# The per-row numbers of two softmaxes combined through scalar operands instead of tensor operands, in a two-layer hybrid encoder

## The chip, the cores and the metric

The kernel runs on one core of a Trainium2 chip, as one program. The metric is the device time of one execution in microseconds; several executions are timed and the median is quoted. The profile is of one further execution. Its span runs from the first to the last instruction that the profiler saw, and its own time is a little longer than its span.

## The reference

A sequence of 1024 tokens of width 1024, with 16 meta tokens put in front (1040 rows, T in the kernel), goes through two layers. The first layer holds two attentions side by side, and the change touches the softmax of both.

```python
# attention A ("MLA", 8 heads): dense, every row sees all 1040 keys
s = einsum('bhqd,bhkd->bhqk', qb, k) * scale
p = softmax(s, axis=-1)
o = einsum('bhqk,bhkd->bhqd', p, v)

# attention B ("SWA", 8 heads, 2 of keys): 16 meta keys and a band of +-128 keys,
# and one learned logit per head, the sink, which takes part in the sum only
p = softmax(concatenate([s_sink, s_meta, s_band], axis=-1), axis=-1)
o_real = p[..., 1:1+N_META] @ v_m + p[..., 1+N_META:] @ v_b
```

The rest of the first layer is an input projection, low-rank projections for attention A, a gate, and an output projection. The second layer is an input projection, a convolution, two recurrent scans and an output projection.

## The kernel before

Everything is float32. A product is made on TensorE (PE) from split operands: each operand is rounded to a shorter type ("hi") and the remainder is kept ("lo"), and three matmuls (lo x hi, hi x lo, hi x hi) go into one sum. So most tensors exist as a pair, and the remainder is always a subtraction on VectorE (DVE), or on GpSimd (POOL) for weights.

The program is written as one sequence, and a scheduler places the instructions on each engine's queue by its own estimate of durations; each queue then runs strictly in the order that was fixed. The stages, by the profile's time: first projections to about 290 us; attention B from 290 to 590 us, with projections of later tiles filling PE in between; gates to 700 us; one half of the output projection, with the first scores of attention A, to 775 us; attention A from 775 to 1140 us; the other half of the output projection; then the second layer from about 1200 us.

**Attention B** (`Unit`, lines 650 to 751) works in 36 units: four pairs of heads by nine blocks of query rows, where the ninth block is the 16 meta rows of both heads in one tile. For each of the two heads of a unit, three matmuls put the scores into PSUM (`sps`), and a custom DVE instruction (L685) scales them, adds the mask, writes `sp` (in the code `pt`) and returns the row maximum in `smx`. `snm` is the negated maximum (L688). Then the exponential of sink minus maximum, `ses`, is made in two steps: a DVE subtraction (L690) and a ScalarE (ACT) exponential (L691). ACT takes the exponential of each head's scores (L694) and sums it into `ssm`. DVE adds `ses` to the sum (L696) and takes the reciprocal (L697). POOL normalises the 16 meta columns into `spm` (L700), DVE the others (L703). PE transposes the result (L718, L721), and then come the products with the values.

**Attention A** (`m_scores`, from line 908; `m_values`, from line 960) works on 8 heads by 9 blocks of rows, in four groups of blocks per head. The scores of one block fill three stretches of PSUM (`px` two, `py` one, L918). DVE takes the maximum of 784 columns and of 256 columns (L924, L925) into two columns of the small tile `mmx`. L926 takes the larger of these two columns and multiplies it by the negated scale of the row, `nsc`. ACT takes the exponential of both parts (L928), each with its sum in a column of `mmx`. L930 adds the two sums, L931 takes the reciprocal, and POOL normalises: L936 the meta columns (`mpm`), L939 the other 1024 (`p`). Then PE transposes `p` (L982), ACT and DVE split the transpose into `pth` (L988) and `ptl` (L989), and PE multiplies them with the values (`av`, L998). For the meta columns the same is `mpr` (L976, L977, L993). The next head is prepared meanwhile (`head_prep`, from line 834): POOL makes `kn` and `rkb` (L844, L845), DVE the remainders `qnl`, `qrl`, `knl`, `kr`, `vl`, `mvmr` (L848, L759, L855, L868), and `yal` when a head's output is split.

Of the kernel before, what the change touches and what calls it, by code (L numbers as in the profile page):

```python
# [10 lines left out]
AF = mybir.ActivationFunctionType  # L11
ALU = mybir.AluOpType
# [29 lines left out]
def trunk_kernel(ctx: ExitStack, tc: tile.TileContext, a: dict, out: bass.AP):  # L42
    nc = tc.nc
# [28 lines left out]
    def row(nm, tag, dt=F32, w=T):  # L72
        if tag == "X":
            return xapool.tile([P, T], dt, tag="X", name=nm)
        return sb["P"].tile([P, w], dt, tag=tag, name=nm, bufs=sb["cnt"][tag])
# [90 lines left out]
    def bank(nm, tag):  # L166
        return sb["ps"].tile([P, 512], F32, tag=tag, name=nm, bufs=sb["pcnt"][tag])
# [88 lines left out]
    for k in range(8):  # L256
        h = row("xh", "X", F32R)
# [68 lines left out]
    for e in range(2):  # L326
        ps = first[3 + e]
        r = row("ckr", "T")
# [48 lines left out]
    for e in range(3):  # L377
        ps = run(proj1(e))
        h = row("cqh", "c", F32R)
        lo = row("cql", "c", F32R)  # L380
        r = row("cqr", "T")
# [84 lines left out]
    for hf in range(2):  # L466
        wu = [split_w(a["uv"][hf, k], (512,), "wv") for k in range(2)]
        for i in range(9):
            c0, m = (0, NM) if i == 8 else (NM + P * i, P)
# [41 lines left out]
    nsc = const.tile([P, 8, 9], F32, name="nsc")  # L511
# [138 lines left out]
    class Unit:  # L650
# [5 lines left out]
        def scores(self):  # L656
            u, i = self.u, self.i
            kh, kl = KV[u // 2, "k"]
            qs, qmeta, sc = QQ[u]
            if i == 8:  # L660
                m, w, nh = 32, 144, 1
                k0, mask, self.blocks = 0, m_meta, [0]
                lhs = [(qmeta[:, 0], qmeta[:, 1])]
                scs = [sc[:32, 16:17]]
                sinks = vec[:32, V_SINKM + u:V_SINKM + u + 1]
            else:
                m, nh = P, 2
                qsl = slice(NM + P * i, NM + P * i + P)
                lhs = [(qs[r][0][:, qsl], qs[r][1][:, qsl]) for r in range(2)]
                scs = [sc[:, 8 * r + i:8 * r + i + 1] for r in range(2)]  # L670
                sinks = vec[:, V_SINK + 2 * u:V_SINK + 2 * u + 2]
                if i == 0:
                    k0, w, mask, self.blocks = 0, 288, m_first, [0, 1]
                elif i == 7:
                    k0, w, mask, self.blocks = 144 * 6, 288, m_mid[:, :288], [6, 7]
                else:
                    k0, w, mask, self.blocks = 144 * (i - 1), 432, m_mid, [i - 1, i, i + 1]
            self.m, self.nh = m, nh
            pt = self.pt = row("sp", "sp", w=864)
            mx = small.tile([P, 2], F32, tag="smx", name="smx")  # L680
            for r in range(nh):
                ps = bank("sps", "s")
                for pi, (q, k) in enumerate(((lhs[r][1], kh), (lhs[r][0], kl), (lhs[r][0], kh))):
                    nc.tensor.matmul(ps[:m, :w], q, k[:, k0:k0 + w], start=pi == 0, stop=pi == 2)
                nc.vector.tensor_tensor_reduce(pt[:m, 432 * r:432 * r + w], ps[:m, :w], mask, scs[r], sinks[:, r:r + 1],  # L685
                                               ALU.add, ALU.max, mx[:m, r:r + 1])
            nm = small.tile([P, 2], F32, tag="snm", name="snm")
            nc.vector.tensor_scalar(nm[:m, :nh], mx[:m, :nh], -1.0, None, ALU.mult)  # L688
            es = small.tile([P, 2], F32, tag="ses", name="ses")
            nc.vector.tensor_sub(es[:m, :nh], sinks, mx[:m, :nh])  # L690
            nc.scalar.activation(es[:m, :nh], es[:m, :nh], AF.Exp)  # L691
            sm = small.tile([P, 2], F32, tag="ssm", name="ssm")
            for r in range(nh):
                nc.scalar.activation(pt[:m, 432 * r:432 * r + w], pt[:m, 432 * r:432 * r + w], AF.Exp,  # L694
                                     bias=nm[:m, r:r + 1], accum_out=sm[:m, r:r + 1])
            nc.vector.tensor_add(sm[:m, :nh], sm[:m, :nh], es[:m, :nh])  # L696
            nc.vector.reciprocal(sm[:m, :nh], sm[:m, :nh])  # L697
            pm = self.pm = swa.tile([P, 2, 96], F32, tag="spm", name="spm", bufs=2)
            for r in range(nh):
                nc.gpsimd.tensor_scalar(pm[:m, r].rearrange("p (a b) -> p a b", a=3),  # L700
                                        pt[:m, 432 * r:432 * r + 32].unsqueeze(1).to_broadcast([m, 3, 32]),
                                        sm[:m, r:r + 1], 1.0, ALU.mult, ALU.mult)
                nc.vector.tensor_scalar(pt[:m, 432 * r + NM:432 * r + w], pt[:m, 432 * r + NM:432 * r + w],  # L703
                                        sm[:m, r:r + 1], None, ALU.mult)
# [203 lines left out]
    def m_scores(h, tiles, res, tag="p", pms=None):  # L908
        q, qq, k, kr = HD[h][:4]
        for i in tiles:  # L910
            c0, m = (0, NM) if i == 8 else (NM + P * i, P)
            s = slice(c0, c0 + m)
            seq = ((q[1], k[0]), (q[0], k[1]), (qq[1], kr), (qq[0], kr), (q[0], k[0]))
            px = psC.tile([P, 1024], F32, tag="px", name="px", bufs=2)
            py = bank("py", "py")
            for dst, d0, a0, a1 in ((px, 240, 0, 272), (px, 512, 272, 784), (py, 0, 784, 1040)):
                for pi, (l, r) in enumerate(seq):
                    nc.tensor.matmul(dst[:m, d0:d0 + a1 - a0], l[:, s], r[:, a0:a1], start=pi == 0, stop=pi == 4)  # L918
                yield 1.0 / (3 * len(tiles))
            mx = small.tile([P, 6], F32, tag="mmx", name="mmx")  # L920
            sc = msc[:m, h, i:i + 1]
            p_ = row("p", tag)
            parts = ((py[:m, 0:256], 784, 1040), (px[:m, 240:1024], 0, 784))
            nc.vector.reduce_max(mx[:m, 0:1], parts[1][0], axis=AX.X)  # L924
            nc.vector.reduce_max(mx[:m, 1:2], parts[0][0], axis=AX.X)  # L925
            nc.vector.scalar_tensor_tensor(mx[:m, 2:3], mx[:m, 0:1], mx[:m, 1:2], nsc[:m, h, i:i + 1], ALU.max, ALU.mult)  # L926
            for z, (ps, b0, b1) in enumerate(parts):
                nc.scalar.activation(p_[:m, b0:b1], ps, AF.Exp, bias=mx[:m, 2:3], scale=sc,  # L928
                                     accum_out=mx[:m, 3 + z:4 + z])
            nc.vector.tensor_add(mx[:m, 5:6], mx[:m, 3:4], mx[:m, 4:5])  # L930
            nc.vector.reciprocal(mx[:m, 5:6], mx[:m, 5:6])  # L931
            if pms is None:
                pm = mla.tile([P, 96], F32, tag="mpm", name="mpm", bufs=6)
            else:
                pm = pms[:, 96 * len(res):96 * len(res) + 96]
            nc.gpsimd.tensor_scalar(pm[:m].rearrange("p (a b) -> p a b", a=3),  # L936
                                    p_[:m, 0:32].unsqueeze(1).to_broadcast([m, 3, 32]),
                                    mx[:m, 5:6], 1.0, ALU.mult, ALU.mult)
            nc.gpsimd.tensor_scalar(p_[:m, NM:T], p_[:m, NM:T], mx[:m, 5:6], 1.0, ALU.mult, ALU.mult)  # L939
            res.append((m, p_, pm))  # L940

    RES = {(0, 0): []}
    early = m_scores(0, GR[0], RES[0, 0], "X", row("pms", "X"))
    for d in range(8):
        ps = parts_c("op")
# [74 lines left out]
    def score_stream():  # L1020
        for h in range(8):
            prep = head_prep(h + 1, kpe, mla) if h < 7 else iter(())
            for gi in range(4):
                if h + gi:
                    res = RES[h, gi] = []
                    yield from m_scores(h, GR[gi], res)
                else:
                    yield from early
                if h + gi:
                    next(prep, None)  # L1030
            for _ in prep:
                pass
# [472 lines left out]
```

## Time and profile before

| | |
|---|---|
| time, median of 3 runs | 1940.13 us (1939.22 to 1945.82) |
| profiled execution, own time | 1936.07 us |
| its span | 1934.3 us |
| PE busy | 1828.5 us, 95% |
| DVE busy | 1278.4 us, 66% |
| ACT busy | 827.9 us, 43% |
| POOL busy | 943.9 us, 49% |
| granted TensorE clock, mean | 0.986 |

In a row of instructions, `x72: 202/220/2376` means 72 instructions with a shortest, a median and a longest duration in ns. In a row of groups, `| 35.8, 534 | 0.7` means 35.8 us busy in all, 534 ns for one on average, and 0.7 us in which the engine sat idle just before them. In a row of the timeline the first two numbers are start and duration in us, and square brackets give the idle time before the instruction and what ended it.

### The profile page before, as it was taken

Reading aid. Unit: us, or ns where it says so; the run is one execution under the profiler, and the core shown is the slowest. Engines: PE = TensorE matmul, PEld = TensorE weight load, DVE = VectorE, ACT = ScalarE, POOL = GpSimd, SP = SyncE. Lnnn points to the kernel's source line nnn. Section 1 sums busy time; section 2 is a strip of 40 time slices with the busy share of each in tenths; the row PEclk is TensorE's granted clock in tenths of the full one; section 3 lists DMA queues with packets and bytes.
Section 4 is the critical chain, followed back from the end, with each engine's and each line's share of the span. In section 5 each row is a group of like instructions: output and inputs, shape, how many; then the busy total and the mean of one; then the engine's idle time right before and its main releaser. Section 6 shows DMA issues by size and latency. Waiting matters only on the chain.

```text
span 1934.3 us, 28455 instructions
## 1 busy us (share of the span) xinstructions
PE 1828.5 (95%) x10822; PEld 1659.4 (86%) x10822; DVE 1278.4 (66%) x1953; ACT 827.9 (43%) x1366; POOL 943.9 (49%) x780
## 2 busy tenths in 40 slices
PE   8999989998999999999999999999999899988999
PEld 7988988888999999788878999988888788876887
DVE  7686358787663432889888753368898989893000
ACT  5455224444342201666666642155656464652000
POOL 5455355535224652544433333358676777655331
PEclk9999999999999999999999999999999999998999
DMA  5256532222223451323221014312222222246521
GB/s 180 73 184 232 132 84 65 64 75 72 78 75 122 143 194 57 113 73 92 69 70 55 18 47 160 106 50 71 82 67 81 84 69 88 66 157 232 183 82 44
DMA packets 111062, 192.77 MB, mean 100 GB/s; under 512 B 32143, under 2 KB 51727, under 8 KB 110926
## 3 DMA queue, kind: packets, MB, share of 16 engines
q1 hardware_dynamic: 110926, 190.96, 31.4%
q8 instruction: 85, 1.39, 0.3%
q14 instruction: 51, 0.42, 0.1%
HBM read 129.86 MB, written 53.06 MB: 95 GB/s over the span
## 4 chain that ended last, share of the span: by engine, by line
PE 53%; DVE 20%; POOL 9%; issue 9%; DMA 5%; ACT 4%; SPq 1%; DVEq 0%; ACTq 0%; POOLq 0%
PE pj L159 10%; PE oo L159 8%; PE pxop L159 6%; PE px L918 4%; PE av L998 4%; PE op L159 3%; PE up L159 3%; PE tp L982 3%; PE vps L426 2%; DVE tz L1243 2%; DMA wr<-in_wg 2%; POOL oz L1253 2%; POOL wl L107 2%; DVE oxc L1167 2%; PE pg L1143 2%
## 5 line engine op out<-in xcount | busy, mean ns | idle before, releaser
L106 POOL TENSOR_SCALAR wh<-wr 128x512 fp32r<-128x512 f32 (+2 forms) x219 | 196.3, 897 | 396.4 <-PE pj L159 99.0
L107 POOL TENSOR_TENSOR wl<-wr,wh 128x512 fp32r<-128x512 f32 (+2 forms) x219 | 352.6, 1610 | 17.5
L159 PE MATMUL pj<-xh,wl 128*128 128x346 f32 (+1 forms) x768 | 251.8, 328 | 12.3 <-DVE wl L107 7.2
L159 PE MATMUL pj<-xl,wh 128*128 128x346 f32 (+1 forms) x768 | 249.3, 325 | 0.7 <-DVE xl L260 0.6
L159 PE MATMUL pj<-xh,wh 128*128 128x346 f32 (+1 forms) x768 | 248.9, 324 | 0.0
L159 PEld LDWEIGHTS pj<-xh,wl 128*128 128x128 f32 x768 | 146.6, 191 | 14.2 <-ACT xh L259 7.1
L159 PEld LDWEIGHTS pj<-xl,wh 128*128 128x128 f32 x768 | 146.7, 191 | 2.2 <-DVE xl L260 2.1
L159 PEld LDWEIGHTS pj<-xh,wh 128*128 128x128 f32 x768 | 146.6, 191 | 0.1
L936 POOL TENSOR_SCALAR mpm<-p,mmx 128x96 f32<-128x96 f32 (+1 forms) x69 | 25.7, 372 | 209.2 <-DVE mmx L931 119.9
L1143 PE MATMUL pu<-h1h,wl 128*128 128x346 f32 (+1 forms) x384 | 125.5, 327 | 0.8 <-POOL wh L106 0.8
L1143 PE MATMUL pu<-h1l,wh 128*128 128x346 f32 (+1 forms) x384 | 124.9, 325 | 0.0
L1143 PE MATMUL pu<-h1h,wh 128*128 128x346 f32 (+1 forms) x384 | 124.8, 325 | 0.0
L988 ACT CAST pth<-tp 128x512 fp32r<-128x512 f32 (+1 forms) x160 | 78.9, 506 | 83.4 <-PE tp L982 82.0
L1294 DVE TENSOR_TENSOR hres<-oo,hres 128x512 f32<-128x512 f32 x16 | 10.6, 687 | 151.6 <-PE oo L159 151.6
L989 DVE TENSOR_TENSOR ptl<-tp,pth 128x512 fp32r<-128x512 f32 (+1 forms) x160 | 91.9, 583 | 23.3 <-ACT pth L988 21.7
L159 PE MATMUL oo<-oyl,wh 128*128 128x512 f32 x256 | 102.3, 400 | 4.4 <-DMA oyl<-s_yl 4.4
L159 PE MATMUL oo<-oyh,wl 128*128 128x512 f32 x256 | 100.3, 401 | 3.3 <-DMA oyh<-s_y 3.3
L159 PE MATMUL oo<-oyh,wh 128*128 128x512 f32 x256 | 102.7, 402 | 0.0
L1143 PE MATMUL pg<-h1h,wl 128*128 128x512 f32 x256 | 101.4, 396 | 0.0
L1143 PE MATMUL pg<-h1h,wh 128*128 128x512 f32 x256 | 101.1, 395 | 0.0
L1143 PE MATMUL pg<-h1l,wh 128*128 128x512 f32 x256 | 100.8, 394 | 0.0
L982 PE MATMUL tp<-ident,p 128*128 128x128 f32 (+1 forms) x576 | 96.2, 274 | 0.0
(446 smaller groups left out, 5564.5 us busy)
## 6 DMA issues: line engine op xcount, KB each, us to landing
wr<-in_w SPq DMA_DIRECT2D x128, 256.0 KB
wr<-in_wo SPq DMA_DIRECT2D x64, 256.0 KB
s_y<-oyh SPq DMA_DIRECT2D x14, 512.0 KB
s_yl<-oyl SPq DMA_DIRECT2D x14, 512.0 KB
oyh<-s_y SPq DMA_DIRECT2D x14, 512.0 KB
oyl<-s_yl SPq DMA_DIRECT2D x14, 512.0 KB
s_g<-gth SPq DMA_DIRECT2D x10, 520.0 KB
xr<-in_x SPq DMA_DIRECT2D x8, 520.0 KB
```

The costliest lines, as they stand in the source:

```text
L106: eng.tensor_scalar(hi[:, :n], raw[:, :n], 1.0, 1.0, ALU.mult, ALU.mult)
L107: eng.tensor_sub(lo[:, :n], raw[:, :n], hi[:, :n].bitcast(F32))
L159: nc.tensor.matmul(t[:, :c1 - c0], w, x[:, c0:c1], start=first and j == 0 and pi == 0, stop=last and j == nt - 1 and pi == 2)
L426: nc.tensor.matmul(ps[:m, :n], s, w, start=j == 0 and pi == 0, stop=j == nt - 1 and pi == 2)
L918: nc.tensor.matmul(dst[:m, d0:d0 + a1 - a0], l[:, s], r[:, a0:a1], start=pi == 0, stop=pi == 4)
L982: nc.tensor.transpose(tp[:, o:o + m], p_[:m, NM + P * (kt + j):NM + P * (kt + j) + P], ident[:m, :m])
L988: nc.scalar.copy(hi[:, :w], tp[:, :w])
L989: nc.vector.tensor_sub(lo[:, :w], tp[:, :w], hi[:, :w].bitcast(F32))
L998: nc.tensor.matmul(av[:, :n], l[:, vs], pts[kt][o][:, j * n:j * n + n], start=kt == 0 and j == 0 and pi == 0, stop=False)
L1143: nc.tensor.matmul(t[:, :c1 - c0], l, r[:, c0:c1], start=hf == 0 and k == 0 and pi == 0, stop=hf == 1 and k == 3 and pi == 2)
L1167: nc.vector.scalar_tensor_tensor(xc[:, 2:T], u[:, 0:T - 2], cw[0], xc[:, 2:T], ALU.mult, ALU.add)
L1243: nc.vector.scalar_tensor_tensor(tz[:, d, :n], av[:, :n], 1.0, tz[:, d, :n], ALU.add, ALU.mult)
```

## The change

In attention B, the sink's exponential is no longer a DVE subtraction and one ACT exponential over both heads' columns. It is one ACT exponential for each head, on the sink's column, with the negated maximum as the bias operand. The sum of `ssm` and `ses` is one `tensor_scalar` for each head, with `ses` as a scalar operand (one value per partition), where it was one `tensor_add` of two tensors with two columns. In attention A, the maximum-and-scale is a `tensor_scalar` with two scalar operands where it was a `scalar_tensor_tensor` with two tensors and one scalar operand, and the sum of the two sums is a `tensor_scalar` where it was a `tensor_add`.

```diff
@@ Unit.scores
             es = small.tile([P, 2], F32, tag="ses", name="ses")
-            nc.vector.tensor_sub(es[:m, :nh], sinks, mx[:m, :nh])
-            nc.scalar.activation(es[:m, :nh], es[:m, :nh], AF.Exp)
+            for r in range(nh):
+                nc.scalar.activation(es[:m, r:r + 1], sinks[:, r:r + 1], AF.Exp, bias=nm[:m, r:r + 1])
...
-            nc.vector.tensor_add(sm[:m, :nh], sm[:m, :nh], es[:m, :nh])
+            for r in range(nh):
+                nc.vector.tensor_scalar(sm[:m, r:r + 1], sm[:m, r:r + 1], es[:m, r:r + 1], None, ALU.add)
@@ m_scores
-            nc.vector.scalar_tensor_tensor(mx[:m, 2:3], mx[:m, 0:1], mx[:m, 1:2], nsc[:m, h, i:i + 1], ALU.max, ALU.mult)
+            nc.vector.tensor_scalar(mx[:m, 2:3], mx[:m, 0:1], mx[:m, 1:2], nsc[:m, h, i:i + 1], ALU.max, ALU.mult)
...
-            nc.vector.tensor_add(mx[:m, 5:6], mx[:m, 3:4], mx[:m, 4:5])
+            nc.vector.tensor_scalar(mx[:m, 5:6], mx[:m, 3:4], mx[:m, 4:5], None, ALU.add)
```

Behind the first edit the changed kernel's lines count one more than before (L696 becomes L697, L926 becomes L927).

Since the scheduler places everything anew, instructions also trade places. On ACT in attention B, in a middle unit of the first pair of heads, this stood before (`ph` and `spmr` belong to the transposes of the unit before, `yt` to the output of the one before that):

```order
L726 CAST ph<-tA 128x512
L729 CAST ph<-tB 128x256
L694 ACTIVATE sp,ssm<-sp,snm 128x432
L691 ACTIVATE ses<-ses 128x2
L694 ACTIVATE sp,ssm<-sp,snm 128x432
L731 CAST spmr<-tB 96x256
L746 COPY yt<-av 128x256
```

and this stands there now:

```order
L727 CAST ph<-tA 128x512
L730 CAST ph<-tB 128x256
L691 ACTIVATE ses<-vec,snm 128x1 x2
L694 ACTIVATE sp,ssm<-sp,snm 128x432 x2
L624 CAST sqh__3429<-qraw 128x1040
L732 CAST spmr<-tB 96x256
L747 COPY yt<-av 128x256
```

The sink's exponential stood between the two heads' exponentials, and is now two instructions ahead of both of them.

On DVE in attention A, where the output of one head is split while the next head is prepared (from 970.9 us in the profile before), this stood before:

```order
L925 TENSOR_REDUCE mmx<-py 128x1
L1016 TENSOR_TENSOR ya<-av,ya 128x256
L926 SCALAR_TENSOR_TENSOR mmx<-mmx,nsc 128x1
L868 TENSOR_TENSOR mvmr<-mvm,mvmr 32x128
L759 TENSOR_TENSOR yal<-ya,yah 128x1040
L924 TENSOR_REDUCE mmx<-px 128x1
L930 TENSOR_TENSOR mmx<-mmx 128x1
L989 TENSOR_TENSOR ptl<-tp,pth 128x272
```

and this stands there now:

```order
L926 TENSOR_REDUCE mmx<-py 128x1
L1017 TENSOR_TENSOR ya<-av,ya 128x256
L927 TENSOR_SCALAR mmx<-mmx,nsc 128x1
L869 TENSOR_TENSOR mvmr<-mvm,mvmr 32x128
L760 TENSOR_TENSOR yal<-ya,yah 128x1040
L925 TENSOR_REDUCE mmx<-px 128x1
L931 TENSOR_SCALAR mmx<-mmx 128x1
L990 TENSOR_TENSOR ptl<-tp,pth 128x272
```

Nothing moved here: the two instructions are exchanged for another kind, and their neighbours are the same. At other places of attention A `mmx` instructions and `ptl` trade places by one or two positions, and on PE some groups of score matmuls and value matmuls do.

## The prediction

> **What bounds the kernel.** I read the page's busy times first, then the busy time by stage, then what PE waits for in the two attentions, then the rows of the four kinds of instruction that the change touches.
>
> ```profile
> PE 1828.5 (95%) x10822; PEld 1659.4 (86%) x10822; DVE 1278.4 (66%) x1953; ACT 827.9 (43%) x1366; POOL 943.9 (49%) x780
> ```
>
> PE is busy for 95% of the span. What the change can give is PE's idle time in the two stages that it touches. In the next rows (stage, sum, and busy time of PE, weight load, DVE, ACT, POOL) the first is attention B and the second attention A.
>
> ```profile
> 290.00:590.00 300.00, 280.87 (x1855) 271.31 (x1854) 217.32 (x567) 133.42 (x368) 127.71 (x151) 0.99 0.27 71
> 775.00:1140.00 365.00, 346.33 (x2386) 301.72 (x2385) 305.78 (x604) 232.37 (x503) 149.45 (x155) 1.00 0.22 66
> ```
>
> PE sits idle for 300.0 - 280.9 = 19.1 us in B and 365.0 - 346.3 = 18.7 us in A, at a granted clock of 0.99 and 1.00. That is the ceiling: 38 us in all, and less by what the change doesn't touch. In A, DVE is busy for 306 of 365 us, so it is next behind PE, and PE's waits there (us in total, times, longest) name it:
>
> ```profile
> PE av L998 <- DVE ptl L989: 8.0, 7, 2.3
> PE py L918 <- ACT p L928: 5.0, 5, 3.1
> PE av L993 <- DVE mpr L977: 2.5, 3, 1.0
> PE px L918 <- DVE kr L855: 1.1, 2, 0.9
> PE av L998 <- DVE ya L1016: 0.9, 1, 0.9
> ```
>
> These add up to 17.5 us in 18 waits. Why DVE is late shows in its own groups: two instructions that make one number per row cost far more than their kind needs.
>
> ```profile
> L926 DVE SCALAR_TENSOR_TENSOR mmx<-mmx,nsc 128x1 f32<-128x1 f32 (+1 forms) x67 | 35.8, 534 | 0.7
> L930 DVE TENSOR_TENSOR mmx<-mmx 128x1 f32<-128x1 f32 (+1 forms) x68 | 18.7, 276 | 22.0 <-ACT p L928 21.8
> L926 DVE SCALAR_TENSOR_TENSOR mmx<-mmx,nsc x72: 202/220/2376, 729.7 to 1136.4; 128x1 f32<-128x1 f32 x64, 16x1 f32<-16x1 f32 x8
> L930 DVE TENSOR_TENSOR mmx<-mmx x72: 138/158/2396, 731.7 to 1138.4; 128x1 f32<-128x1 f32 x64, 16x1 f32<-16x1 f32 x8
> L931 DVE RECIPROCAL mmx<-mmx x72: 139/155/166, 731.8 to 1138.6; 128x1 f32<-128x1 f32 x64, 16x1 f32<-16x1 f32 x8
> ```
>
> The median is 0.22 and 0.16 us, but single ones take 2.4 us; the reciprocal, with one input, never takes more than 0.17. Above their medians the two cost 35.8 - 67 x 0.220 = 21.1 us and 18.7 - 68 x 0.158 = 8.0 us of DVE in this stage. The timeline around the longest wait of PE shows what they wait for:
>
> ```profile
> 968.42 2.42 POOL L844 TENSOR_TENSOR kn<-kn,rkb 128x1040 f32<-128x1040 f32 x1 [2.05 <-DMA rkb<-d_rk]
> 968.50 2.36 DVE L930 TENSOR_TENSOR mmx<-mmx 128x1 f32<-128x1 f32 x1
> 971.56 2.39 POOL L845 TENSOR_TENSOR rkb<-kpe,rkb 128x1040 f32<-128x1040 f32 x1
> 971.62 2.35 DVE L926 SCALAR_TENSOR_TENSOR mmx<-mmx,nsc 128x1 f32<-128x1 f32 x1
> 974.00 1.19 DVE L868 TENSOR_TENSOR mvmr<-mvm,mvmr 32x128 fp32r<-32x128 f32 x1
> 974.06 0.56 ACT L928 ACTIVATE p<-py,mmx,msc 128x256 f32<-128x256 f32 x1 [1.27 <-DVE mmx L926]
> 974.77 0.38 PE L918 MATMUL py<-knh,qnl 128*128 128x256 f32 x1 [3.14 <-ACT p L928]
> ```
>
> Both DVE instructions end within 0.03 us of a POOL instruction that began just before them (968.42 + 2.42 = 970.84 against 970.86; 973.95 against 973.97). A DVE instruction with two inputs in SBUF is held until POOL's instruction is over. Two further rows show who is not held, over the same stages in which POOL works:
>
> ```profile
> L989 DVE TENSOR_TENSOR ptl<-tp,pth x155: 369/673/693, 774.3 to 1139.5; 128x512 fp32r<-128x512 f32 x91, 128x272 fp32r<-128x272 f32 x64
> L685 DVE CUSTOM_DVE_ANT_0 sp<-sps,masks,vec x68: 409/722/731, 290.7 to 582.3; 128x432 f32<-128x432 f32 x48, 128x288 f32<-128x288 f32 x16, 32x144 f32<-32x144 f32 x4
> ```
>
> `ptl` has one input in PSUM and one in SBUF and never passes 0.69 us. L685 reads PSUM, one SBUF tensor and two columns as scalar operands, and never passes 0.73. So a scalar operand does not bring the hold, and the new forms, with one SBUF tensor and one or two scalar operands, should not be held.
>
> **The change part by part, attention A.** L926 and L930 become `tensor_scalar`, 72 each, on the same queue with the same waits. Unheld, each costs between 0.14 us (L931's shortest) and 0.22 us (L926's median), so at most 72 x (0.22 - 0.16) = 4 us of DVE is added to L930's kind, against 29 us of hold that goes; I take 0. What the 29 us are worth is read from PE's waits, not from DVE's sum, since most of it lies under PE's work.
>
> The waits for `p` come behind an L926; where that one is held, as above, the wait goes whole, and I take 4.5 of 5.0 us, leaving the smallest of the five. For `mpr` a row stands for the three:
>
> ```profile
> 1017.86 2.40 DVE L930 TENSOR_TENSOR mmx<-mmx 128x1 f32<-128x1 f32 x1 [0.30 <-ACT p L928]
> 1020.96 0.39 PE L993 MATMUL av<-mpr,mvmr 96*128 96x256 f32 x1 [0.93 <-DVE mpr L977]
> ```
>
> The hold of 2.4 us is longer than the wait behind it: 2.2 of 2.5. For `ptl` two cases differ:
>
> ```profile
> 883.43 2.34 DVE L930 TENSOR_TENSOR mmx<-mmx 128x1 f32<-128x1 f32 x1
> 886.17 0.40 PE L998 MATMUL av<-ptl,vh 128*128 128x272 f32 x1 [1.11 <-DVE ptl L989]
> 886.69 2.45 POOL L845 TENSOR_TENSOR rkb<-kpe,rkb 128x1040 f32<-128x1040 f32 x1
> 887.50 1.67 DVE L926 SCALAR_TENSOR_TENSOR mmx<-mmx,nsc 128x1 f32<-128x1 f32 x1
> 889.19 1.18 DVE L868 TENSOR_TENSOR mvmr<-mvm,mvmr 32x128 fp32r<-32x128 f32 x1
> 891.15 0.39 PE L998 MATMUL av<-ptl,vh 128*128 128x256 f32 x1 [2.33 <-DVE ptl L989]
> ```
>
> The 1.11 us go with L930's hold. Of the 2.33 us only part goes: freed, L926 ends at 887.7, but L868 behind it has two SBUF inputs too and now meets the same L845, which runs until 889.14. The hold passes to the next instruction. So of 8.0 us I take half, 4.0. The waits for `kr` and `ya` follow wide two-input instructions that stay: 0. Together 4.5 + 2.2 + 4.0 = 10.7 us. PE, running earlier, will meet some other wait (DVE stays at over 75% busy, and L868 shows the kind), so I give a quarter back: **-8 us**, with the ends 0 and -17.5.
>
> The new order on PE and DVE of A (single places up or down) I cost at 0: it changes what is next in line, not the amount of work; PE's busy time covers it. Without that cover it is worth single waits of the size shown, 1 to 3 us either way.
>
> **Attention B.** The hold matters less here, and the chain of the unit gets other steps. PE waits for it in this row, and these are the parts (ACT and DVE groups, then two neighbours on ACT):
>
> ```profile
> PE tA L718 <- DVE sp L703: 7.3, 10, 1.6
> L694 ACT ACTIVATE sp<-sp,snm 128x432 f32<-128x432 f32 x48 | 31.1, 649 | 32.2 <-DVE ses L690 32.2
> L694 ACT ACTIVATE sp<-sp,snm 128x288 f32<-128x288 f32 x16 | 8.4, 529 | 4.6 <-DVE ses L690 2.1 <-DVE ssc L638 2.1 <-DVE snm L688 0.4
> L691 ACT ACTIVATE ses<-ses 128x2 f32<-128x2 f32 x32 | 6.2, 193 | 1.6 <-DVE ses L690 1.6
> L690 DVE TENSOR_TENSOR ses<-vec,smx 128x2 f32<-128x2 f32 x32 | 5.7, 179 | 0.0
> L696 DVE TENSOR_TENSOR ssm<-ssm,ses 128x2 f32<-128x2 f32 x32 | 7.1, 221 | 19.3 <-ACT sp L694 19.2
> 353.02 0.19 ACT L691 ACTIVATE ses<-ses 128x2 f32<-128x2 f32 x1
> 353.12 0.52 ACT L694 ACTIVATE sp<-sp,snm 128x288 f32<-128x288 f32 x1
> ```
>
> An exponential with a bias operand costs, by the two widths, (649 - 529)/144 = 0.83 ns per column and 529 - 288 x 0.83 = 290 ns besides. The next instruction starts 0.09 us before the end of the one ahead (353.02 + 0.19 against 353.12). So each of the two new sink exponentials puts 0.29 - 0.09 = 0.20 us ahead of the first score exponential, 0.40 in all. In return the 0.10 us between the two exponentials goes, and the subtraction L690 (0.18 at most, less where it overlaps) no longer stands before ACT. Net +0.12 to +0.23 us to the end of the second exponential; the second of the two additions adds up to 0.15 on DVE. I take +0.25 us per unit. Exposed in the ten units in which PE waits for L703: +2.5 us; under cover everywhere it would be 0, and exposed in all 36 units with 0.15 more it would be 36 x 0.4 = +14. L696's mean is 0.06 above L930's median of the same kind, 32 x 0.06 = 2 us of hold, of which I take a quarter: -0.5. Together **+2 us**.
>
> **The sum.** -8 + 2 = -6 us, on the profiled execution's 1936.07 us: 1930. That execution was 4.06 us under the median of the three runs, so against the median the same step gives 1940.13 - 6 = 1934 us, -0.3%. About 0.5%, 9.7 us, is what can be told from no change.
>
> **A rule weighed.** L685 shows scalar operands beside PSUM, not a `tensor_scalar` in SBUF, and this row is a `tensor_scalar` that is held:
>
> ```profile
> L688 DVE TENSOR_SCALAR snm<-smx x36: 130/160/1032, 291.6 to 582.9; 128x2 f32<-128x2 f32 x32, 32x1 f32<-32x1 f32 x4
> ```
>
> With two columns it reaches 1.03 us. [...] No row of this trace shows a 128x1 `tensor_scalar`.
>
> **The rivals.**
> - *The new form is held all the same*, as L688 is. Then A gives 0 and B costs its 2 us: 1942. For it: L688. Against it: L688 has two columns, and its four 32x1 forms are too few to tell. Chance 0.15.
> - *All of the waits go* and nothing takes their place: -17.5 + 2 = -15.5, 1925. For it: L926's hold goes ahead of nearly every `ptl`, and what DVE gains (29 us) is more than PE's waits. Against it: L868 at 889.19. With a gain over 12 in A the time is under 1930.4. Chance 0.30.
> - *Slower: attention B's chain is exposed.* The two sink exponentials stand ahead of the scores' in an in-order queue; if PE waits for L703 in most units and not in ten, 36 x 0.4 = +14 us, with -8 from A: 1946. It decides when the delay per exposed unit times their number passes A's gain, 20 units at 0.4 us. Against it: 26 units show no such wait now. Chance 0.12.
> - *The forecast*, 1930.4 to 1940: 0.43.
>
> Faster by over 0.5%: the second case and a little of the forecast, 0.34. Slower by over 0.5%: half of the third case and an order that goes wrong, 0.08. The rest, 0.58, can't be told from no change. The range goes from 1922 (the second case with some of B's idle time) to 1945 (the third).
>
> **What will show it.** Right: L927 and L931 (the two instructions of A after the change) with no duration over 0.3 us, DVE's busy time in A down by 25 us or more, PE's wait for `p` under 1 us, and L869 or `yal` longer than before. B: two L691 of about 0.29 us ahead of each pair of L694, and PE's wait for L704 up by 1 to 3 us. Wrong: L927 still at up to 2.4 us (first rival), or PE's idle time in B up by 8 us (third), or PE waits in A that stay near 17 us under other names.

## The result, and the profile after

The changed kernel takes 1927.05 us (median of 6 runs, 1925.13 to 1931.39), against 1939.68 us for the kernel before on the same chip. The ratio is 0.9936, with a 95% interval from 0.9917 to 0.9954: faster by 12.6 us. The forecast was faster by 6 us, so the direction came as forecast and the size lies between it and the rival in which all of the waits go. The profiled execution took 1926.06 us, its span 1924.3 us, at the same mean clock of 0.986 as before.

The busy times of the page, and the two stages by the same windows as before:

```profile
PE 1826.4 (95%) x10822; PEld 1659.6 (86%) x10822; DVE 1266.3 (66%) x1949; ACT 836.7 (43%) x1398; POOL 952.5 (49%) x780
290.00:590.00 300.00, 282.31 (x1852) 272.67 (x1851) 221.83 (x567) 142.41 (x399) 126.56 (x150) 0.98 0.26 71
775.00:1140.00 365.00, 355.43 (x2473) 313.14 (x2472) 295.12 (x612) 235.05 (x509) 155.18 (x158) 1.00 0.23 67
```

PE did 2473 matmuls in attention A's 365 us, where it did 2386 before. B's window holds nearly as many as it did. To compare equal work in A, the next two rows are cut at the same instructions, the first of the kernel before and the second of the changed one:

```profile
775.00:1152.80 377.80, 359.13 (x2480) 313.94 (x2479) 310.24 (x612) 235.94 (x510) 152.11 (x158) 1.00 0.22 64
775.70:1141.20 365.50, 355.93 (x2479) 313.73 (x2478) 295.18 (x612) 234.90 (x509) 155.97 (x158) 1.00 0.22 66
```

The same work takes 377.8 - 365.5 = 12.3 us less. PE's idle time falls from 18.7 to 9.6 us and its busy time by 3.2 us, in one execution of each kernel. Up to A's first instruction the changed kernel is 0.7 us later, and behind A it takes 1.6 us more, so the span is 10.0 us shorter: A gives all of the gain.

The four kinds of instruction that the change touched, with what stands beside them (durations as minimum, median and maximum in ns):

```profile
L927 DVE TENSOR_SCALAR mmx<-mmx,nsc x72: 252/266/275, 730.3 to 1124.8; 128x1 f32<-128x1 f32 x64, 16x1 f32<-16x1 f32 x8
L931 DVE TENSOR_SCALAR mmx<-mmx x72: 192/214/216, 732.3 to 1126.9; 128x1 f32<-128x1 f32 x64, 16x1 f32<-16x1 f32 x8
L691 ACT ACTIVATE ses<-vec,snm x68: 277/293/308, 292.5 to 584.4; 128x1 f32<-128x1 f32 x64, 32x1 f32<-32x1 f32 x4
L697 DVE TENSOR_SCALAR ssm<-ssm,ses x68: 194/214/217, 293.3 to 585.7; 128x1 f32<-128x1 f32 x64, 32x1 f32<-32x1 f32 x4
L688 DVE TENSOR_SCALAR snm<-smx x36: 132/162/1562, 292.3 to 583.7; 128x2 f32<-128x2 f32 x32, 32x1 f32<-32x1 f32 x4
```

None of the 212 one-column `tensor_scalar` is held: their longest is 0.28 us, where the old forms in A reached 2.4. Among the instructions of one or two columns only `snm` (L688), with two, still is, up to 1.56 us. PE's waits in A are now these:

```profile
PE av L999 <- DVE ptl L990: 6.0, 6, 1.6
PE px L919 <- DVE kr L856: 1.2, 2, 1.0
PE av L999 <- DVE ya L1017: 0.7, 1, 0.7
PE px L919 <- DVE knl L760: 0.5, 1, 0.5
PE py L919 <- ACT p L929: 0.5, 2, 0.3
```

They add up to 8.9 us, against 17.5 before. The wait for `p` is down from 5.0 to 0.5 and the one for `mpr` is gone. The wait for `ptl`, the largest, kept 6.0 of its 8.0 us, and the timeline of two such waits shows why:

```profile
878.43 3.22 POOL L845 TENSOR_TENSOR kn<-kn,rkb 128x1040 f32<-128x1040 f32 x1 [2.07 <-DMA rkb<-d_rk]
879.76 2.03 DVE L869 TENSOR_TENSOR mvmr<-mvm,mvmr 32x128 fp32r<-32x128 f32 x1
882.90 0.39 PE L999 MATMUL av<-ptl,vh 128*128 128x272 f32 x1 [1.45 <-DVE ptl L990]
...
1013.18 2.45 POOL L846 TENSOR_TENSOR rkb<-kpe,rkb 128x1040 f32<-128x1040 f32 x1
1013.28 3.45 DVE L760 TENSOR_TENSOR yal<-ya,yah 128x1040 fp32r<-128x1040 f32 x1
1018.13 0.39 PE L999 MATMUL av<-ptl,vh 128*128 128x272 f32 x1 [1.58 <-DVE ptl L990]
```

`mvmr` ends at 881.79, 0.14 us behind POOL's `kn`, and `yal` takes 3.45 us where its shortest takes 1.22. In the second case POOL's `rkb` ends at 1015.63, and `yal` ends 1.10 us behind it, about the time that it takes unheld. The hold moved to the next two-input instruction in DVE's queue. POOL is held in turn: its `mpm` (L937), 0.34 us long at 1007.77, takes 1.33 us at 1015.61, beside this `yal`, and POOL's busy time on the page rose from 943.9 to 952.5 us. The groups of DVE over the equal work (busy us, then mean ns) show how much, first before and then after:

```profile
L759 DVE TENSOR_TENSOR yal<-ya,yah 128x1040 fp32r<-128x1040 f32 x7 | 11.0, 1566 | 1.0 <-ACT yah L758 0.9
L848 DVE SCALAR_TENSOR_TENSOR qnl<-qn,gqk,qnh 128x1040 fp32r<-128x1040 f32 x7 | 9.3, 1335 | 0.4 <-ACT qnh L847 0.4
L759 DVE TENSOR_TENSOR knl<-kn,knh 128x1040 fp32r<-128x1040 f32 x7 | 8.6, 1235 | 0.0
L868 DVE TENSOR_TENSOR mvmr<-mvm,mvmr 32x128 fp32r<-32x128 f32 x7 | 4.0, 574 | 0.2
```

```profile
L927 DVE TENSOR_SCALAR mmx<-mmx,nsc 128x1 f32<-128x1 f32 (+1 forms) x67 | 17.9, 267 | 0.8
L931 DVE TENSOR_SCALAR mmx<-mmx 128x1 f32<-128x1 f32 (+1 forms) x68 | 14.1, 208 | 21.2 <-ACT p L929 20.7
L760 DVE TENSOR_TENSOR yal<-ya,yah 128x1040 fp32r<-128x1040 f32 x7 | 12.8, 1831 | 0.7 <-ACT yah L759 0.6
L849 DVE SCALAR_TENSOR_TENSOR qnl<-qn,gqk,qnh 128x1040 fp32r<-128x1040 f32 x7 | 11.8, 1688 | 1.0 <-ACT qnh L848 1.0
L760 DVE TENSOR_TENSOR knl<-kn,knh 128x1040 fp32r<-128x1040 f32 x7 | 10.0, 1432 | 0.1
L869 DVE TENSOR_TENSOR mvmr<-mvm,mvmr 32x128 fp32r<-32x128 f32 x7 | 6.3, 907 | 0.2
```

L927 and L931 fell from 35.8 + 18.7 to 17.9 + 14.1 us, by 22.5. The four two-input ones grew from 32.9 to 40.9 us, by 8.0. That leaves 14.5 of the 15.1 us by which DVE's busy time in A fell.

### The profile page after: what moved, and what is told of

The parts are those of the page before. It is cut to its first block, busy times and chain, and to the rows that moved or that the text cites. A ratio compares the mean times of both kernels' runs of the same rounds, so it can differ in the third digit from the quotient of the medians.

```text
span 1924.3 us, 28457 instructions
## 1 busy us (share of the span) xinstructions
PE 1826.4 (95%) x10822; PEld 1659.6 (86%) x10822; DVE 1266.3 (66%) x1949; ACT 836.7 (43%) x1398; POOL 952.5 (49%) x780
## 4 chain that ended last, share of the span: by engine, by line
PE 54%; DVE 18%; POOL 10%; issue 8%; DMA 5%; ACT 4%; SPq 2%; DVEq 0%; POOLq 0%; ACTq 0%
PE pj L159 10%; PE oo L159 8%; PE pxop L159 6%; PE px L919 5%; PE av L999 4%; PE op L159 3%; PE tp L983 3%; PE up L159 3%; DMA wr<-in_wg 2%; DVE tz L1244 2%; POOL oz L1254 2%; PE py L919 2%; POOL wl L107 2%; DVE oxc L1168 2%; PE pg L1144 2%
## 5 line engine op out<-in xcount | busy, mean ns | idle before, releaser
L107 POOL TENSOR_TENSOR wl<-wr,wh 128x512 fp32r<-128x512 f32 (+2 forms) x219 | 351.4, 1605 | 17.5
L159 PE MATMUL pj<-xh,wl 128*128 128x346 f32 (+1 forms) x768 | 251.5, 328 | 12.6 <-DVE wl L107 6.7
L937 POOL TENSOR_SCALAR mpm<-p,mmx 128x96 f32<-128x96 f32 (+1 forms) x69 | 29.7, 431 | 193.5 <-DVE mmx L932 105.0
L990 DVE TENSOR_TENSOR ptl<-tp,pth 128x512 fp32r<-128x512 f32 (+1 forms) x160 | 92.0, 584 | 29.9 <-ACT pth L989 29.1
```

The lines of the kernel that those rows point to most:

```text
L107: eng.tensor_sub(lo[:, :n], raw[:, :n], hi[:, :n].bitcast(F32))
L159: nc.tensor.matmul(t[:, :c1 - c0], w, x[:, c0:c1], start=first and j == 0 and pi == 0, stop=last and j == nt - 1 and pi == 2)
L990: nc.vector.tensor_sub(lo[:, :w], tp[:, :w], hi[:, :w].bitcast(F32))
```

## The experiments

Three accounts of the gain were set against each other. By the first, the hold: the new form escapes DVE's wait for POOL, and nothing else matters. By the second, the order: new instructions make the scheduler place the work differently, and that is the gain. By the third, attention B has a part in it, for better or worse. All ratios are to the kernel before on the same chip, with 95% intervals. The last column is the time from the first to the last start of the instruction that scales the maximum (L926 before), the length of A's softmaxes in the one profiled execution. That of the kernel before was 3.6 us under its median, so its 406.7 is on the short side.

| kernel | median us | ratio | A's softmaxes us |
|---|---|---|---|
| before | 1938.8 to 1940.6 | 1 | 406.7 |
| changed | 1927.05 | 0.9936 [0.9917, 0.9954] | 394.5 |
| only A's two edits | 1927.08 | 0.9933 [0.9921, 0.9945] | 399.0 |
| only B's edits | 1940.26 | 1.0007 [0.9999, 1.0016] | 415.1 |
| two columns | 1941.33 | 1.0005 [0.9993, 1.0018] | 412.0 |
| only A's maximum | 1934.31 | 0.9968 [0.9956, 0.9980] | 405.1 |
| only A's sum | 1937.10 | 0.9989 [0.9980, 0.9998] | 406.5 |
| three columns | 1952.76 | 1.0068 [1.0054, 1.0081] | 422.8 |
| one column, zeroed tile | 1945.95 | 1.0036 [1.0020, 1.0052] | 421.5 |
| A, `mvmr` on POOL | 1928.09 | 0.9935 [0.9922, 0.9948] | 398.3 |
| A, `mvmr` and `yal` on POOL | 1927.78 | 0.9942 [0.9930, 0.9954] | 394.1 |
| A, `spm` on ACT | 1931.92 | 0.9954 [0.9940, 0.9967] | 399.2 |
| A, all three moved | 1934.52 | 0.9980 [0.9964, 0.9996] | 394.1 |
| A, `mvmr` and six `yal` on POOL | 1925.26 | 0.9926 [0.9911, 0.9942] | 394.9 |

**Only attention A's edits.** The kernel before with these two lines.

```diff
-scalar_tensor_tensor(mx[:m, 2:3], mx[:m, 0:1], mx[:m, 1:2], nsc[:m, h, i:i + 1], ALU.max, ALU.mult)
+tensor_scalar(mx[:m, 2:3], mx[:m, 0:1], mx[:m, 1:2], nsc[:m, h, i:i + 1], ALU.max, ALU.mult)
...
-tensor_add(mx[:m, 5:6], mx[:m, 3:4], mx[:m, 4:5])
+tensor_scalar(mx[:m, 5:6], mx[:m, 3:4], mx[:m, 4:5], None, ALU.add)
```

> Only the two edits of attention A. Theory H (the hold behind POOL's instructions is what went): all of the gain is here, 9 to 13 us under before, PE's waits in A at about 9 us. Rival B (attention B's edits have their part in the gain): 5 us or less under before. If B's edits cost what the prediction gave them, this kernel is 2 us faster than the changed one.

1927.08 us, ratio 0.9933: the whole gain. The instruction is as short as in the changed kernel:

```profile
L926 DVE TENSOR_SCALAR mmx<-mmx,nsc x72: 251/265/274, 727.1 to 1126.1; 128x1 f32<-128x1 f32 x64, 16x1 f32<-16x1 f32 x8
PE av L998 <- DVE ptl L989: 8.5, 9, 1.6
```

PE's waits in A add up to 11.5 us here, not to the 9 expected. The wait for `p` is 0.5 us and the one for `mpr` is gone, as in the changed kernel, but the wait for `ptl` is as long as before the change. So the gain does not rest on the wait for `ptl`.

**Only attention B's edits.** The kernel before with the edits in `Unit`.

```diff
-tensor_sub(es[:m, :nh], sinks, mx[:m, :nh])
-activation(es[:m, :nh], es[:m, :nh], AF.Exp)
+activation(es[:m, r:r + 1], sinks[:, r:r + 1], AF.Exp, bias=nm[:m, r:r + 1])   # each r
...
-tensor_add(sm[:m, :nh], sm[:m, :nh], es[:m, :nh])
+tensor_scalar(sm[:m, r:r + 1], sm[:m, r:r + 1], es[:m, r:r + 1], None, ALU.add)   # each r
```

> Only the two edits of attention B. Theory H: within 2 us of before, since PE's idle time in B stays at 18 to 20 us. Prediction: 2 us slower. Rival B: 5 us or more faster.

1940.26 us, ratio 1.0007, with an interval from 0.2 us faster to 3.1 us slower: no difference that can be told. PE's wait for the probabilities in B is 6.8 us, where it was 7.3:

```profile
PE tA L719 <- DVE sp L704: 6.8, 9, 1.8
L927 DVE SCALAR_TENSOR_TENSOR mmx<-mmx,nsc x72: 199/219/2376, 726.4 to 1141.5; 128x1 f32<-128x1 f32 x64, 16x1 f32<-16x1 f32 x8
```

With the run before it, a part of B in the gain falls, and so does an exposed chain of many microseconds. A loss of up to 3 us is not excluded by the times, but PE's wait shows no sign of one.

**Two columns in place of one.** The same `tensor_scalar`, on two adjacent columns, of which the second is not used. It keeps the operation, its scalar operands and its place. The small tile grows from 6 to 14 columns for it.

```diff
-tensor_scalar(mx[:m, 2:3], mx[:m, 0:1], mx[:m, 1:2], nsc[:m, h, i:i + 1], ALU.max, ALU.mult)
+tensor_scalar(mx[:m, 8:10], mx[:m, 0:2], mx[:m, 1:2], nsc[:m, h, i:i + 1], ALU.max, ALU.mult)
...
-tensor_scalar(mx[:m, 5:6], mx[:m, 3:4], mx[:m, 4:5], None, ALU.add)
+tensor_scalar(mx[:m, 11:13], mx[:m, 3:5], mx[:m, 4:5], None, ALU.add)
```

> The changed kernel, but the two tensor_scalar of attention A write two columns where one is used, so that they are as wide as L688, which the trace shows held. The order on PE is that of the changed kernel but for a few neighbours. Theory H: the hold is back, L927 reaches 2 us or more, and the time goes back to about 1936 to 1941. Rival O (the new order, not the hold, brought the gain): time stays at 1925 to 1930, whatever L927 takes. Rival W (tensor_scalar is not held at any width, L688 was held for another reason): L927 stays under 0.3 us and the time too.

1941.33 us, ratio 1.0005. The hold is back, in instructions whose median is only 0.01 to 0.02 us higher, and with it PE's waits:

```profile
L927 DVE TENSOR_SCALAR mmx<-mmx,nsc x72: 271/289/2424, 728.7 to 1140.7; 128x2 f32<-128x2 f32 x64, 16x2 f32<-16x2 f32 x8
L931 DVE TENSOR_SCALAR mmx<-mmx x72: 207/227/2446, 730.7 to 1142.8; 128x2 f32<-128x2 f32 x64, 16x2 f32<-16x2 f32 x8
PE av L999 <- DVE ptl L990: 6.9, 7, 3.1
PE py L919 <- ACT p L929: 6.8, 8, 3.1
PE av L994 <- DVE mpr L978: 2.9, 2, 2.6
```

The order of the queues is nearly that of the changed kernel: in the two profiles two matmuls on PE, one cast on ACT and a few neighbours at one place on DVE stand elsewhere, and nothing on POOL. So the gain went with the hold and not with the order, and the second account falls. This is the run that carries the explanation.

**Each of A's edits alone.** Of the first diff above, the upper pair of lines alone (L926), and then the lower pair alone (L930).

> Only L926's edit (the larger maximum times the scale). Its hold above the median was 21 of 29 us of DVE in A, and all waits of PE for p and half of those for ptl stand behind it. Theory H: 6 to 9 us under before, L930 still at up to 2.4 us. Rival O: anything, not in proportion to the hold.

> Only L930's edit (the sum of the two sums). Its hold above the median was 8 of 29 us of DVE in A, with two of PE's largest waits for mpr and ptl behind it. Theory H: 2 to 6 us under before, and together with the run of L926's edit alone (6 us) about what both give (13 us); L926 still at up to 2.4 us. If more than half of the 13 us is missing from the sum, the two holds feed each other.

L926 alone gives a ratio of 0.9968, which is 6.2 us, and L930 alone 0.9989, 2.1 us: 8.3 us together, where both at once give 13. The instruction that stays in its old form is held as it was: L930 takes 300 ns on average in the first kernel (276 before), L926 509 in the second (534 before). Here is that instruction in each, with PE's largest wait:

```profile
L930 DVE TENSOR_TENSOR mmx<-mmx x72: 138/158/2287, 729.3 to 1134.3; 128x1 f32<-128x1 f32 x64, 16x1 f32<-16x1 f32 x8
PE av L998 <- DVE ptl L989: 9.2, 9, 2.9
```

```profile
L926 DVE SCALAR_TENSOR_TENSOR mmx<-mmx,nsc x72: 203/220/2401, 732.4 to 1138.9; 128x1 f32<-128x1 f32 x64, 16x1 f32<-16x1 f32 x8
PE av L998 <- DVE ptl L989: 9.3, 7, 2.8
```

With one of them still held, PE's waits in A add up to 16.0 or 14.2 us, against 17.5 before and 11.5 with both of A's edits. The wait for `ptl` alone does not tell them apart: 9.2 and 9.3 us, and 8.5 with both. That the two edits help each other is likely, since with one alone the chain still meets a hold. But the 5 us that are missing from the sum are little more than the intervals of the three runs leave (2.3, 2.3 and 1.7 us either way).

**Three columns.** An odd width, to see whether two columns were held for being even. Two columns that it reads are not written otherwise, so the first six columns of the small tile are zeroed, by one more DVE instruction per block.

```diff
+nc.vector.memset(mx[:m, 0:6], 0.0)
-tensor_scalar(mx[:m, 2:3], mx[:m, 0:1], ...)
+tensor_scalar(mx[:m, 8:11], mx[:m, 0:3], ...)
```

> As the run with two columns, but three columns are written (and the six columns of the small tile are set to zero first, one more short DVE instruction per tile). Theory W1 (only a width that can be halved brings the hold): L927 under 0.4 us, time 1926 to 1931. Rival W2 (any width over one brings it): L927 up to 2.4 us, time 1936 to 1943.

```profile
L928 DVE TENSOR_SCALAR mmx<-mmx,nsc x72: 276/289/2301, 728.8 to 1151.6; 128x3 f32<-128x3 f32 x64, 16x3 f32<-16x3 f32 x8
```

Three columns are held too, up to 2.3 us: an odd width does not escape. Its time, 1952.76 us, can't be read as the hold's price alone, because of the zeroing. So a control had the same zeroing and one column (`mx[:m, 8:9]` from `mx[:m, 0:1]`):

> The control for the run with three columns: the same zeroing of the small tile, the same order on ACT and POOL and nearly on PE, but one column is written. That run came out 13 us slower than before instead of 0. If its excess over the run with two columns (11 us) belongs to the zeroing, which waits for POOL to let go of the small tile, and to the order that it brings, this kernel is 8 to 15 us faster than the run with three columns (1952.8), at 1938 to 1945. If three columns as such are dearer, it is at 1927 to 1930.

```profile
L928 DVE TENSOR_SCALAR mmx<-mmx,nsc x72: 251/266/275, 729.5 to 1151.0; 128x1 f32<-128x1 f32 x64, 16x1 f32<-16x1 f32 x8
PE av L1000 <- DVE ptl L991: 17.7, 10, 3.4
```

It is not held, and yet it takes 1945.95 us, 19 more than the changed kernel and just over the range expected for it. The zeroing itself is 0.063 us of DVE. But it must wait until POOL has read the tile's former content (DVE sat idle for 13.1 us in 11 places for that), and the order around it changed. PE's wait for `ptl` rose to 17.7 us. Between the two zeroing kernels the medians differ by 6.8 us and the intervals do not meet, but the two profiled executions have the same span (1950.2 and 1950.6 us). That three columns are held is shown; what the hold costs there is not.

**Taking away what the hold passes on to.** The prediction named `mvmr` and `yal` as the next to be held. Four kernels with A's edits move two-input work away from DVE or POOL. The first makes `mvmr` on POOL, the second `yal` too:

```diff
-nc.vector.tensor_sub(vmr[64:96], vm[64:96], vmr[64:96].bitcast(F32))
+nc.gpsimd.tensor_sub(vmr[64:96], vm[64:96], vmr[64:96].bitcast(F32))
...
-YH[h], YL[h] = split(y, "ya", "X")
+YH[h], YL[h] = split(y, "ya", "X", eng=nc.gpsimd)
```

> Attention A's two edits, and the subtraction of mvmr (two inputs in SBUF, 32x128, up to 2.0 us when held) on POOL instead of DVE. If the hold that passed to it costs PE: 1 to 3 us under the kernel with attention A's edits alone (1927.1), so 1924 to 1926. If it merely passes on to the next two-input instruction, or POOL's queue is late for it: no change.

> As the run before, and the remainder yal of each head's output (1024 columns and meta, held up to 3.4 us) on POOL as well. Two of the remaining waits of PE for ptl, 1.4 and 1.6 us, stand behind yal: 2 to 5 us under 1927.1 if nothing else is hurt; slower than that if POOL's 2.4 us for it delay the normalisation p, which PE's transposes wait for.

Neither differs from A's edits alone. With `mvmr` on POOL a new wait comes up on DVE's in-order queue, since the zeroing of the next `mvm` must wait for POOL's reading of the last one. With `yal` on POOL too, PE's wait for `ptl` falls from 8.5 to 4.8 us and A's softmaxes take 394.1 us in place of 399.0, but at A's end PE waits for the slower `yal` of the last head (the first row is of the first kernel):

```profile
L862 DVE MEMSET mvm<- 96x128 f32 x4 | 0.7, 165 | 6.5 <-POOL mvmr L868 6.5
```

```profile
PE av L998 <- DVE ptl L989: 4.8, 5, 3.0
PE pxop L159 <- POOL yal L759: 2.5, 1, 2.5
L759 POOL TENSOR_TENSOR yal<-ya,yah x8: 2372/2423/3382, 823.1 to 1143.0; 128x1040 fp32r<-128x1040 f32 x8
```

POOL takes 2.42 us for a `yal`, DVE 1.24. The last kernel of this study left the last two heads' `yal` on DVE:

> Attention A's two edits, the mvmr subtraction on POOL for all heads and yal on POOL for the heads 0 to 5 only. In the kernel with yal of all heads on POOL, PE waits 2.5 us for the last yal at the end of attention A (the row 'PE pxop L159 <- POOL yal L759: 2.5, 1, 2.5'), and the time is 1927.8. Theory of the late yal: that wait goes and nothing takes its place, so 1925.3, 2 to 3 us under the changed kernel, and the stretch from the first to the last L926 stays near 394 us. Rival, nothing more to gain: the wait goes, but the time stays within 1 us of 1927, because what is left in PE's way are waits for ptl (4.8 us there) that come with any order.

The wait is gone, and the time is 1925.26 us (1919.52 to 1927.02), ratio 0.9926. That is the size that the late `yal` would give, and the lowest median of all. But its interval, 0.9911 to 0.9942, covers the changed kernel's ratio, so that it beats the changed kernel is not shown.

**The holding side in B.** POOL's normalisation of the meta columns (`spm`) was moved to ACT, with A's edits, and then together with `mvmr` and `yal`:

```diff
-nc.gpsimd.tensor_scalar(pm[:m, r]..., pt[:m, ...], sm[:m, r:r + 1], 1.0, ALU.mult, ALU.mult)
+nc.scalar.activation(pm[:m, r]..., pt[:m, ...], AF.Identity, scale=sm[:m, r:r + 1])
```

> Attention A's two edits, and in attention B the normalised meta columns spm made by ACT instead of POOL, so that L703 (a tensor_scalar of 272 or 416 columns, up to 1.3 us when held) is no longer held by them. PE waits 6.8 us for L703 in B. Theory H: 2 to 5 us under the kernel with attention A's edits alone. If ACT's queue is late for it: no change or slower.

> As the run before, with mvmr and yal of attention A on POOL as well. The lowest of all if the two act apart: 1922 to 1926.

Both are slower than A's edits alone, by 4.8 and 7.4 us in the medians. The loss lies in B. In the first, PE waits for the probabilities (L703) 12.1 us, where it is 7.3 with A's edits alone, and single L703 take 2.5 us where the longest was 1.3:

```profile
PE tA L718 <- DVE sp L703: 12.1, 10, 2.1
L703 DVE TENSOR_SCALAR sp<-sp,ssm x68: 264/431/2542, 293.5 to 592.1; 128x416 f32<-128x416 f32 x48, 128x272 f32<-128x272 f32 x16, 32x128 f32<-32x128 f32 x4
290.00:590.00 300.00, 279.70 (x1813) 270.00 (x1812) 214.54 (x559) 153.43 (x431) 98.85 (x81) 0.97 0.26 70
```

The row of the same window with A's edits alone is this:

```profile
290.00:590.00 300.00, 281.52 (x1868) 271.77 (x1866) 219.25 (x571) 134.64 (x371) 128.56 (x151) 0.99 0.26 71
```

The two longest L703 are held by other work of POOL: they run beside its L398 of 2.5 us, end 0.23 us behind it, and PE waits 2.07 us behind each. The granted clock is also lower, 0.97 against 0.99. In slices of 1 us it falls to 0.50 in five stretches of about 3.4 us, where A's edits alone have one such stretch. By an estimate that takes half of their length as lost, five stretches cost 8.6 us against full clock, and one costs 1.7. The difference of 6.9 us is as large as the whole difference between the two profiled executions, whose spans are 1931.8 and 1925.3 us, so the clock can account for most of what is lost there. Each of the five begins within a pause of PE or at most 1.4 us behind one, and three of these pauses are waits for L703. But not every pause is followed by one (the 2.33 us that end at 891.15 in the profile before the change are not), so that the longer waits brought them is not shown.

## Why the prediction was right, and where its sizes were off

**The mechanism.** The step that carried the forecast, that scalar operands don't bring the hold and that the new forms would not be held, is shown by the durations of L927 and L931, at most 0.28 and 0.22 us, and by the run with two columns, which puts the hold back and loses the whole gain. The first rival, that the new form is held all the same, is wrong for one column and right for two and three. That a DVE instruction with two inputs in SBUF is held until POOL's is over was put wider than the rows have it: before the change `kr` (L855) takes its median 1.24 us at 877.95, and POOL's `p` (L939), begun 0.07 us ahead of it, takes 2.21 us where its median is 1.13.

**Term A, -8 us, measured -12.3 on equal work.** Its parts: the wait for `p` gave 4.5 us of the 4.5 forecast, and the wait for `mpr` 2.5 of 2.2. The wait for `ptl` gave 2.0 where 4.0 stood, and nothing in the run of A's edits alone. The hold passed on as the prediction had it, to L869 and also to `yal` and `qnl`, and three quarters of that wait stayed. The quarter given back on top of that did not come: a new wait for `knl` is 0.5 us, where 2.7 us were set aside. So the listed waits fell by 8.6 us; that this is close to the 8 is luck, since the two misses cancel. The sum of A was mis-sized elsewhere: "PE's busy time covers it" took the busy time as fixed, and it fell by 3.2 us for the same matmuls. Why is not settled. In the two profiled executions it is not the granted clock, which is halved once in A in each, for about 3.4 us (0.50 from 976 to 978 us before, from 925 to 928 us after). Over many executions the clock is part of the answer at most: among 73 timed executions of the kernel before, the time falls by 0.94 us per 0.001 of mean clock, and the 22 executions of the four kernels that have A's edits, B as before and `spm` on POOL had a mean clock of 0.9849 against 0.9837, which makes 1.1 us of their 12.8. Among the executions at a clock of 0.984 the means are 1939.4 us (19 of them) and 1927.5 us (4 of them).

**The price of the new forms, taken as 0.** It was between 0.14 and 0.22 us by the rows, and came to 0.27 for L927 and 0.21 for L931. So L927 went over its upper bound, since the nearest rows had at most one scalar operand in SBUF. 67 x (0.267 - 0.220) + 68 x (0.208 - 0.158) = 6.5 us of DVE, and DVE's busy time in A fell by 15 us, not by the 25 or more that the prediction asked for: 29.1 of hold, less 6.5 for the form and 8.0 passed on. That this costs little is what the prediction had said: it lies under PE's work.

**Term B, +2 us, measured between 0 and 3.** The price per instruction was right. The sink exponential takes 0.293 us, 0.29 forecast, and two of them put 352.87 - 352.48 = 0.39 us ahead of the first score exponential, where 0.40 stood:

```profile
352.48 0.48 ACT L691 ACTIVATE ses<-vec,snm 128x1 f32<-128x1 f32 x2
352.87 0.53 ACT L694 ACTIVATE sp<-sp,snm 128x288 f32<-128x288 f32 x1
```

What failed is the step from the price to PE: "exposed in the ten units in which PE waits for L703" did not happen. The wait went from 7.3 to 6.8 us, where the prediction's own sign was a rise of 1 to 3. With B's edits alone the time moved by 0.0007 of itself, 1.4 us, and the interval from -0.2 to +3.1 us does not exclude the 2 us; only their cause, the longer wait, is not there. The 0.5 us for L696's hold may have come. The third rival, an exposed chain worth 14 us, falls with the same run.

**The rule weighed.** That a scalar operand does not bring the hold was drawn from L685 and weighed against L688, a `tensor_scalar` that is held with two columns, up to 1.03 us before the change. The rows now tell by width: one column takes at most 0.28 us, two columns of the same form reach 2.45 us, and three reach 2.30. Why one column alone escapes, no run shows.

**The total.** The misses had the same sign: 4 us in A, and up to 2 us in B, make -12 where -6 stood. The 1927 us lie under the forecast's own stretch of 1930.4 to 1940, and a gain of over 0.5% had been given a chance of 0.34, against 0.58 for a time that can't be told from before. So the mechanism and the direction were right, and the size came out larger. The rival "all of the waits go" came close in time, 1925, by luck: half of the waits stayed.

## What to carry to other kernels

Look for tiny two-input DVE instructions whose longest duration is many times their median while POOL works in SBUF (here 2.4 us against 0.22 and 0.16). With one column, a `tensor_scalar` with the second tensor as scalar operand costs about 0.05 us more and was held in none of these runs (0.28 us at most); with two or three columns it is held just the same (up to 2.45 and 2.30 us). Change all such instructions of a chain together, since the hold moves to others (here two-input instructions of the same queue grew by 8.0 us), and count the gain from the waits of the engine that bounds, not from DVE's busy time.

## What was not expected of the hardware

Each scalar operand from SBUF seems to cost DVE about 0.05 us. With 128x1, the addition of two tensors has a median of 0.158 us, the `tensor_scalar` with one such operand 0.214 and with two 0.266; the `scalar_tensor_tensor` with one has 0.220. And a kernel that zeroes a small tile, 0.063 us of work each time, takes 19 us longer than the changed kernel. The zeroing stands in an in-order queue and waits for POOL to let go of the tile, 13.1 us in all; the order around it changed too, and the two were not told apart.
